# A hybrid convolution and retention layer on one core: filler work put in another order, copies and buffers split finer

## The chip, the cores and the metric

The kernel runs on one core of a Trainium2 chip. The metric is the time of one execution in microseconds on the device; the time of a kernel is the median of its runs. The kernel before took 969.17 us (three runs, 967.22 to 969.35).

## What is computed

One layer of a decoder over 1024 tokens of width 1024. A modulated RMS norm makes u; one input projection makes the inputs of a convolution branch and of a retention branch; both meet in one output projection. Cut to what matters here:

```python
u = _rmsnorm(h, norm_g[l]) * (1.0 + scale) + shift
proj = u @ w_in[l]          # conv_a, conv_bp, conv_gate, q, k, v, ret_gate
a = conv_a * jax.nn.sigmoid(conv_bp)
a = _causal_depthwise_conv(a, conv_w[l], conv_b[l])     # 31 taps
a = jax.nn.silu(_layernorm(a, conv_ln_g[l], conv_ln_b[l]))
a = a @ conv_pw[l]
y_conv = a * jax.nn.silu(conv_gate)
r = _retention_chunkwise(_rotary(q), _rotary(k) * (RET_QK_DIM ** -0.5), v)   # 4 heads
r = _head_groupnorm(r, ret_gn_g[l], ret_gn_b[l])
y_ret = r * jax.nn.silu(ret_gate)
y = jnp.concatenate([y_conv, y_ret], axis=-1) @ w_out[l]
return _rmsnorm(h + gate * y, final_g)
```

## The kernel before

All large products run in float32 as three matmuls (`mm3`, L81 to 84): each operand is split into a rounded high part (`split`, L69: a cast on ScalarE) and the remainder (L71: a subtraction on VectorE, or on GpSimd where the call names it), and high by high, high by low and low by high are added up in PSUM.

The stages, with their times in the profile:

1. Up to about 495 us: the norm and the input projection in 21 pairs of blocks, with the 31 convolution taps (L271, VectorE) behind them. The convolution's result goes to DRAM (`d_y`), and GpSimd adds it up over channels into `ysum` (L278).
2. To 535: the first values, for heads 0 and 1 (L512 to 531): eight tiles `t` of 128 tokens, each 24 matmuls of 512 columns (`values_ps`, tiles `ps_v`), with the weights split on GpSimd. The results are copied to SBUF (ScalarE for t < 6, VectorE for 6 and 7) and written to `d_v` by DMAs on GpSimd's queue.
3. To about 700: retention, four heads of four chunks (`retention`, L601 to 707). A chunk loads q, k, sg and v, splits them (tiles `qc`, `kc`, `vc`, with h and l for the parts), transposes k (`kp`), makes scores (`sp`), masks them (`sm`), splits those (`sh`, `sl`), makes outputs (`op`) and the state's update (`up`, then `state`, `sth`, `stl`), and normalises (`ob`, `rs`, `rn`, `tp`). Each step waits for another engine, so other work stands between the chunks to fill TensorE:
   - `ln_squares` (L551 to 569), the first half of the convolution's layer norm: two matmuls with a matrix of ones give the mean from `ysum` (`mu`), ScalarE makes `negmu`, and eight times a tile of `d_y` is loaded, `negmu` added (VectorE), written back, squared (ScalarE) and added to `ysum` (VectorE). Two buffers `yt` carry it.
   - `values` (L590), the second values, for heads 2 and 3: eight tiles again, from weights `w_v[1]` that come in four loads of 512 KB (`load_w`: `raw_v`, `hi_v`, `lo_v`).
   - `ln_scale` (L571 to 586): column sums of `ysum` (`var`), then `rstd` on VectorE, its power on GpSimd (L577), eight diagonal tiles `rs_d` on VectorE (L583), matmuls with ones that spread them over the partitions (`rb`, L584), and copies into `rbs`.
   - `norm_z` (L709), eight tiles: load, multiply by `rbs`, SiLU, split into `zh` and `zl`, the operand of the pointwise projection (`pointwise`, L730, tiles `ps_pw`).
4. To 961: the pointwise projection, then the output projection (L768 to 856), which adds for each tile of tokens a half that comes from retention (`w_r`) and a half that comes from the convolution (`w_c`). The first halves of two tiles run before the `w_c` weights are loaded.

After head 0 stand `ln_squares` and four tiles of second values, after head 1 the other four, then `ln_scale` and the eight `norm_z`. That is the order in the code; the order on each engine is made by a scheduler, which places each instruction by priority and readiness (loads of a chunk are raised by `LOADS_EARLIER`, taps lowered by `TAPS_LATER`); each engine then takes its instructions one after the other.

Of the kernel before, what the change touches and what calls it, by code (L numbers as in the profile page):

```python
# [7 lines left out]
F32 = mybir.dt.float32  # L8
# [4 lines left out]
P = 128  # L13
# [4 lines left out]
TT = S // P  # L18
# [2 lines left out]
EPS = 1e-6  # L21
TAPS_LATER = 3000
LOADS_EARLIER = 800
PAD_SW = 24
PAD_W = 88
CH = 256
NCH = S // CH
HALF = 512
EARLY = (8, 0, 9, 1)
HK = KT // 2  # L30
# [17 lines left out]
def hybrid_layer(ctx: ExitStack, tc: tile.TileContext, x, vec, c_row, ada_ss, ada_g, adab_g, w_e, w_s, w_p, w_v,  # L48
                 w_pw, w_out, final_g, cs, masks, kc, ident, out):
    nc = tc.nc  # L50
# [5 lines left out]
    mmp = ctx.enter_context(tc.tile_pool(name="mm", bufs=4, space=bass.MemoryType.PSUM))  # L56
# [16 lines left out]
    def load_w(src, shape, name, pool, eng=None):  # L73
        raw = pool.tile(shape, F32, tag="raw", name=f"raw_{name}", bufs=2)
        nc.sync.dma_start(raw, src)
        hi = pool.tile(shape, F32R, tag="hi", name=f"hi_{name}")
        lo = pool.tile(shape, F32R, tag="lo", name=f"lo_{name}")
        split(hi, lo, raw, eng)
        return hi, lo
# [211 lines left out]
    def values_ps(t, ws, name):  # L291

        ps = mmp.tile([P, HALF], F32, tag="mm", name=f"ps_{name}{t}")
        sl = slice(t * P, (t + 1) * P)
        for k in range(KT):
            mm3(ps, uh[k][:, sl], ul[k][:, sl], *ws[k], k == 0, k == KT - 1)
        return ps
# [77 lines left out]
    with tc.tile_pool(name="one", bufs=1, reuse_waits="tile") as op_, \  # L375
# [140 lines left out]
        ws = []  # L516
        for k in range(KT):
# [2 lines left out]
            hi, lo = (t[:, k % HK] for t in ((th[2], tl[2]), (th[3], th[4]))[k // HK])  # L520
            split(hi, lo, raw, nc.gpsimd)
            ws.append((hi, lo))
        for t in range(0, TT, 2):
            vs = op_.tile([P, 2, HALF], F32, tag="ro", name=f"vs0{t}", bufs=2)
            for i in range(2):
                ps = values_ps(t + i, ws, "v0")
                if t + 2 < TT:
                    nc.scalar.copy(vs[:, i], ps)
                else:
                    nc.vector.tensor_copy(vs[:, i], ps)  # L530
            values_out(0, t, vs, nc.gpsimd)
    one_ctx.close()
    conv_ctx.close()
# [6 lines left out]
    with tc.tile_pool(name="ret", bufs=1, reuse_waits="tile") as rp, \  # L540
# [10 lines left out]
        def ln_squares():  # L551

            negmu = const.tile([P, S], F32, tag="sig", name="negmu")
            for i in range(2):
                sl = slice(i * HALF, (i + 1) * HALF)
                mu = mmp.tile([P, HALF], F32, tag="mm", name=f"mu{i}")
                nc.tensor.matmul(mu, ones_t, ysum[:, sl], start=True, stop=True)
                nc.scalar.mul(negmu[:, sl], mu, -1.0 / D)
            for m in range(KT):
                yt = fo.tile([P, S], F32, tag="yt", name=f"ys{m}", bufs=2)  # L560
                nc.sync.dma_start(yt, d_y[m])
                nc.vector.tensor_tensor(yt, yt, negmu, op=ADD)
                nc.sync.dma_start(d_y[m], yt)
                if m == 0:
                    nc.scalar.activation(ysum, yt, AF.Square)
                else:
                    sq = fo.tile([P, S], F32, tag="xh", name=f"sq{m}", bufs=2)
                    nc.scalar.activation(sq, yt, AF.Square)
                    nc.vector.tensor_tensor(ysum, ysum, sq, op=ADD)
# [16 lines left out]
            return rbs  # L586

        w_v1 = []

        def values(ts):  # L590

            if not w_v1:
                for j in range(4):
                    hi, lo = load_w(w_v[1, j], [P, 2, HALF], f"v1{j}", wpool)
                    w_v1.extend((hi[:, i], lo[:, i]) for i in range(2))
            for t in ts:
                vs = rp.tile([P, 1, HALF], F32, tag="vs", name=f"vs{t}", bufs=3)
                nc.scalar.copy(vs[:, 0], values_ps(t, w_v1, "v1"))
                values_out(1, t, vs, nc.scalar)

        def retention(h):  # L601
# [4 lines left out]
            for c in range(NCH):  # L606
# [3 lines left out]
                def chunk(tag, src):  # L610
                    hi = rp.tile([P, 2, CH], F32R, tag=tag + "h", name=f"{tag}h{n}", bufs=2)
                    lo = rp.tile([P, 2, CH], F32R, tag=tag + "l", name=f"{tag}l{n}", bufs=2)
                    split(hi, lo, src)
                    return hi, lo

                def load_c(tag, src):
                    t = rp.tile([P, 2, CH], F32, tag=tag, name=f"{tag}{n}", bufs=2)
                    with tc.high_priority(offset=LOADS_EARLIER):
                        nc.sync.dma_start(t, src)
                    return t  # L620

                q, k = (load_c("qk"[i], d_qk[i, h][:, :, ts]) for i in range(2))
                sg = load_c("sg", d_sg[2 * h:2 * h + 2, :, ts].rearrange("d p s -> p d s"))
                vh, vl = chunk("vc", load_c("v", d_v[h // 2, :, 2 * c:2 * c + 2, h % 2 * 2 * P:(h % 2 + 1) * 2 * P]))
                if c < NCH - 1:

                    kth = rp.tile([P, 2, 2 * P], F32R, tag="kth", name=f"kth{n}", bufs=2)
# [10 lines left out]

                kh, kl = chunk("kc", k)
                qh, ql = chunk("qc", q)  # L640


                sp = rps.tile([P, 3 * P], F32, tag="sp", name=f"sp{n}")
# [76 lines left out]
        for h in range(H):  # L720
            retention(h)
            if h == 0:
                ln_squares()
            if h < 2:
                values(range(h * HK, (h + 1) * HK))
            if h == 1:
                rbs = ln_scale()
                for m in range(KT):
                    zh[m], zl[m] = norm_z(m)
    def pointwise(m):  # L730
        ps = unit(*load_w(w_pw[m], [P, KT, P], f"pw{m}", wpool), zh, zl, f"pw{m}")
        cg = fo.tile([P, S], F32, tag="xh", name=f"cgl{m}", bufs=2)
        nc.sync.dma_start(cg, d_cg[m])
        for i in range(2):
            sl = slice(i * HALF, (i + 1) * HALF)
            nc.vector.tensor_tensor(cg[:, sl], ps[i], cg[:, sl], op=MUL)
        nc.sync.dma_start(d_yc[m], cg)
# [13 lines left out]
    with tc.tile_pool(name="fin", bufs=1, reuse_waits="tile") as fp, \  # L751
# [23 lines left out]
                    not start and k == KT - 1)  # L775

        def both(t):
            return [fps.tile([P, HALF], F32, tag="o", name=f"ps_o{t}_{i}") for i in range(2)]

        def half(ps, w, y, start):  # L780
            for k in range(KT):
# [36 lines left out]

        halves2 = [slice(0, HALF), slice(HALF, D)]
        first = []  # L820
        for t in range(2):
            ps = both(t)
            half(ps, w_r, load_y(d_yr, t, "yr"), True)
            first.append(ps)
        w_c = [load_r(f, big, "big", 17) for f in range(KT)]
        for t in range(TT - 1):
            if t < 2:
                ps = first[t]
            else:
                ps = both(t)  # L830
                half(ps, w_r, load_y(d_yr, t, "yr"), True)
            half(ps, w_c, load_y(d_yc, t, "yc"), False)
            if t == 0:
                for k in range(KT):
                    gate_step(k)
                agb = fo.tile([P, D], F32, tag="yt", name="agb", bufs=2)
                nc.sync.dma_start(agb, adab_g.broadcast_to([P, D]))
                for i in range(2):
                    sl = slice(i * HALF, (i + 1) * HALF)
                    gp = mmp.tile([P, HALF], F32, tag="mm", name=f"gp{i}")  # L840
                    nc.tensor.matmul(gp, ones_t, gate[:, sl], start=True, stop=True)
                    nc.vector.tensor_tensor(gate[:, sl], gp, agb[:, sl], op=ADD)
            finish(t, [(lambda q=q: q, sl) for q, sl in zip(ps, halves2)])
# [99 lines left out]
```

## Time and profile before

| | |
|---|---|
| median of three runs | 969.17 us (967.22 to 969.35) |
| the profiled execution | 970.08 us |
| its span, first to last instruction | 968.3 us |
| mean granted TensorE clock | 0.988 |
| TensorE busy | 937.2 us (97% of the span) |
| VectorE busy | 745.3 us (77%) |
| ScalarE busy | 412.2 us (43%) |
| GpSimd busy | 389.8 us (40%) |
| moved by DMA | 154.95 MB, 160 GB/s |

The busy share is a mean over all stages. A row of a window says how much of a stretch an engine was busy and which clock TensorE was granted in it (1.00 is full speed). A row of a timeline says when an instruction began, how long it took, and in brackets how long its engine had been idle before it and which instruction of which engine released it. Matmuls are pipelined: the time from one to the next is shorter than what a row gives for one. PE is TensorE, DVE VectorE, ACT ScalarE, POOL GpSimd, SP SyncE.

### The profile page before, as it was taken

To read this page: it belongs to the slowest core of one execution; us is meant where nothing else is said; L and a number is where in the kernel's file an instruction comes from. 1 tells how busy PE (TensorE), PEld (TensorE's weight loads), DVE (VectorE), ACT (ScalarE), POOL (GpSimd) and SP (SyncE) were. 2 spreads that over 40 slices of the span, in tenths; PEclk is the share of its full clock that TensorE was granted. 3 is DMA by queue.
4 is the path that set the end of the run, shared out by engine and by line. 5 is a ranking of instruction groups with operands and counts; after the bars stand their busy time and mean duration, and the time that the engine had idled before them with its cause. 6 is when DMAs were issued, how large, how long until landed. Compare 5 with 4: busy or idle time off the path is not lost.

```text
span 968.3 us, 12531 instructions
## 1 busy us (share of the span) xinstructions
PE 937.2 (97%) x4496; PEld 784.5 (81%) x4496; DVE 745.3 (77%) x928; ACT 412.2 (43%) x676; POOL 389.8 (40%) x358
## 2 busy tenths in 40 slices
PE   7999999999999999999999899989999999999996
PEld 5788888888888888888888688877788887888886
DVE  6999989899999999999799786687875344523322
ACT  7775433433434334343430575677634333311201
POOL 3004987877887798878550111121022100000000
PEclk9999999999999999999999899989999999999998
DMA  9924242333334444443434799555775486432111
GB/s 348 331 78 133 75 144 88 118 88 104 125 121 138 133 127 132 134 141 97 154 117 163 267 332 308 179 165 200 240 290 176 157 279 221 147 106 87 65 44 44
DMA packets 84673, 154.95 MB, mean 160 GB/s; under 512 B 6657, under 2 KB 43265, under 8 KB 83330
## 3 DMA queue, kind: packets, MB, share of 16 engines
q1 hardware_dynamic: 81986, 147.07, 45.9%
q0 software_dynamic: 1040, 3.67, 1.0%
q10 hardware_dynamic: 1584, 3.41, 0.9%
q8 instruction: 35, 0.57, 0.2%
q14 instruction: 28, 0.23, 0.1%
HBM read 107.99 MB, written 46.14 MB: 159 GB/s over the span
## 4 chain that ended last, share of the span: by engine, by line
PE 78%; DVE 10%; DMA 5%; issue 3%; ACT 2%; POOL 1%; POOLq 0%; DVEq 0%; ACTq 0%
PE pa L83 7%; PE pa L84 7%; PE pa L82 7%; DVE y L271 4%; PE ps_o L83 4%; PE ps_o L84 4%; PE ps_o L82 4%; PE pb L83 4%; PE pb L82 4%; PE pb L84 4%; PE ps_pw L82 2%; PE ps_pw L84 2%; PE ps_pw L83 2%; DMA wo<-w_out 2%; PE pd L84 2%
## 5 line engine op out<-in xcount | busy, mean ns | idle before, releaser
L271 DVE SCALAR_TENSOR_TENSOR yp<-a,vec_t,yp 128x1024 f32<-128x1024 f32 x210 | 269.7, 1284 | 6.7 <-ACT yp L269 2.7
L334 POOL TENSOR_TENSOR pl<-pr,ph 128x512 fp32r<-128x512 f32 x63 | 84.7, 1345 | 59.7 <-ACT ph L333 59.5
L334 POOL TENSOR_TENSOR pl_s<-sm_s,ph_s 128x512 fp32r<-128x512 f32 x63 | 85.4, 1356 | 36.6 <-ACT ph_s L333 35.1
L333 ACT CAST ph_s<-sm_s 128x512 fp32r<-128x512 f32 x63 | 39.1, 622 | 95.8 <-PE pa L83 80.3
L333 ACT CAST ph<-pr 128x512 fp32r<-128x512 f32 x63 | 39.1, 622 | 79.7 <-PE pa L83 45.4
L806 POOL TENSOR_TENSOR fr<-fr,mhalf 128x1 f32<-128x1 f32 x7 | 3.8, 547 | 168.0 <-DVE fr L805 168.0
L691 POOL TENSOR_TENSOR rs<-mv,kc_t 128x2 f32<-128x2 f32 x16 | 6.2, 390 | 158.7 <-DVE mv L688 133.8
L82 PE MATMUL pb<-uh,ph_s 128*128 128x512 f32 x168 | 65.4, 389 | 0.0
L84 PE MATMUL pb<-uh,pl_s 128*128 128x512 f32 x168 | 65.4, 389 | 0.0
L82 PE MATMUL pa<-th,ph_s 128*128 128x512 f32 x168 | 65.4, 389 | 0.0
L83 PE MATMUL pb<-ul,ph_s 128*128 128x512 f32 x168 | 65.4, 389 | 0.0
L84 PE MATMUL pa<-th,pl_s 128*128 128x512 f32 x168 | 65.4, 389 | 0.0
L83 PE MATMUL pa<-tl,ph_s 128*128 128x512 f32 x168 | 65.4, 389 | 0.0
L346 POOL TENSOR_TENSOR sm_s<-pr,pr 128x512 f32<-128x512 f32 x42 | 57.2, 1362 | 17.3 <-DMA pr<-w_p 10.1
L83 PE MATMUL ps_pw<-zl,hi_pw 128*128 128x512 f32 x128 | 50.4, 394 | 2.2 <-DVE zl L71 2.2
L84 PE MATMUL ps_pw<-zh,lo_pw 128*128 128x512 f32 x128 | 50.6, 395 | 0.0
L82 PE MATMUL ps_pw<-zh,hi_pw 128*128 128x512 f32 x128 | 48.0, 399 | 1.9 <-ACT zh L70 1.7
L271 DVE SCALAR_TENSOR_TENSOR y<-a,vec_t,y 128x1024 f32<-128x1024 f32 x30 | 44.1, 1469 | 6.9 <-ACT y L269 6.1
L797 DVE TENSOR_TENSOR g<-ps_o,gate 128x512 f32<-128x512 f32 x14 | 9.5, 691 | 49.7 <-PE ps_o L84 49.7
L83 PE MATMUL ps_o<-wol,hi_yc 128*128 128x512 f32 x112 | 43.8, 391 | 0.1
L83 PE MATMUL ps_o<-wol,hi_yr 128*128 128x512 f32 x112 | 43.7, 393 | 0.0
L84 PE MATMUL ps_o<-woh,lo_yc 128*128 128x512 f32 x112 | 43.6, 390 | 0.0
(447 smaller groups left out, 2792.9 us busy)
## 6 DMA issues: line engine op xcount, KB each, us to landing
pr<-w_p SPq DMA_DIRECT2D x84, 256.0 KB, 2.7
aw<-ada_ss SPq DMA_DIRECT2D x8, 1024.0 KB, 8.1
d_qk<-ro SPq DMA_DIRECT2D x16, 512.0 KB, 3.3
wo<-w_out SPq DMA_DIRECT2D x16, 512.0 KB, 4.7
xt<-x SPq DMA_DIRECT2D x8, 512.0 KB, 6.9
d_sg<-o SPq DMA_DIRECT2D x16, 256.0 KB, 2.6
sg<-d_sg SPq DMA_DIRECT2D x16, 256.0 KB, 3.5
v<-d_v SPq DMA_DIRECT2D x16, 256.0 KB, 3.4
```

The costliest lines, as they stand in the source:

```text
L82: nc.tensor.matmul(ps, lh, rh, start=start, stop=False, skip_group_check=more)
L83: nc.tensor.matmul(ps, lh, rl, start=False, stop=False, skip_group_check=more)
L84: nc.tensor.matmul(ps, ll, rh, start=False, stop=stop, skip_group_check=more)
L271: nc.vector.scalar_tensor_tensor(acc, ap[:, j:j + S], col(V_CW, m * CW + j), acc, op0=MUL, op1=ADD)
L333: nc.scalar.copy(hi, src)
L334: nc.gpsimd.tensor_tensor(lo, src, hi.bitcast(F32), op=SUB)
L346: nc.gpsimd.tensor_tensor(out, a, b, op=op)
L691: nc.gpsimd.tensor_tensor(rs, mv[:, :, 1], kc_t[:, K_G2 + 2 * h:K_G2 + 2 * h + 2], op=MUL)
L797: nc.vector.tensor_tensor(g[:, :n], ps(), gate[:, sl], op=MUL)
L806: nc.gpsimd.tensor_tensor(r, r, mhalf[:, 0:1], op=ALU.pow)
```

## The change

- The first values are copied tile by tile into single tiles with five buffers (before: pairs with two), so eight writes of 256 KB take the place of four of 512 KB.
- The weights of the second values are loaded and split where the function is defined, ahead of retention, and their lo parts are made on GpSimd.
- After head 0 one tile of second values stands ahead of `ln_squares`, three behind it. After head 1 one tile stands ahead of `ln_scale`, three behind it, then come the `norm_z`.
- In a chunk the values are split after keys and queries.
- The first halves of three output tiles run ahead of the second halves' weights (before two), and the output's PSUM tiles alternate between two pools.

```diff
--- before.py
+++ after.py
@@ -21,6 +21,7 @@
 EPS = 1e-6
 TAPS_LATER = 3000
 LOADS_EARLIER = 800
+AHEAD = 3
 PAD_SW = 24
 PAD_W = 88
 CH = 256
@@ -520,14 +521,13 @@
             hi, lo = (t[:, k % HK] for t in ((th[2], tl[2]), (th[3], th[4]))[k // HK])
             split(hi, lo, raw, nc.gpsimd)
             ws.append((hi, lo))
-        for t in range(0, TT, 2):
-            vs = op_.tile([P, 2, HALF], F32, tag="ro", name=f"vs0{t}", bufs=2)
-            for i in range(2):
-                ps = values_ps(t + i, ws, "v0")
-                if t + 2 < TT:
-                    nc.scalar.copy(vs[:, i], ps)
-                else:
-                    nc.vector.tensor_copy(vs[:, i], ps)
+        for t in range(TT):
+            vs = op_.tile([P, 1, HALF], F32, tag="plb", name=f"vs0{t}", bufs=5)
+            ps = values_ps(t, ws, "v0")
+            if t + 2 < TT:
+                nc.scalar.copy(vs[:, 0], ps)
+            else:
+                nc.vector.tensor_copy(vs[:, 0], ps)
             values_out(0, t, vs, nc.gpsimd)
     one_ctx.close()
     conv_ctx.close()
@@ -586,13 +586,12 @@
             return rbs
 
         w_v1 = []
+        for j in range(4):
+            hi, lo = load_w(w_v[1, j], [P, 2, HALF], f"v1{j}", wpool, nc.gpsimd)
+            w_v1.extend((hi[:, i], lo[:, i]) for i in range(2))
 
         def values(ts):
 
-            if not w_v1:
-                for j in range(4):
-                    hi, lo = load_w(w_v[1, j], [P, 2, HALF], f"v1{j}", wpool)
-                    w_v1.extend((hi[:, i], lo[:, i]) for i in range(2))
             for t in ts:
                 vs = rp.tile([P, 1, HALF], F32, tag="vs", name=f"vs{t}", bufs=3)
                 nc.scalar.copy(vs[:, 0], values_ps(t, w_v1, "v1"))
@@ -621,7 +620,7 @@
 
                 q, k = (load_c("qk"[i], d_qk[i, h][:, :, ts]) for i in range(2))
                 sg = load_c("sg", d_sg[2 * h:2 * h + 2, :, ts].rearrange("d p s -> p d s"))
-                vh, vl = chunk("vc", load_c("v", d_v[h // 2, :, 2 * c:2 * c + 2, h % 2 * 2 * P:(h % 2 + 1) * 2 * P]))
+                v = load_c("v", d_v[h // 2, :, 2 * c:2 * c + 2, h % 2 * 2 * P:(h % 2 + 1) * 2 * P])
                 if c < NCH - 1:
 
                     kth = rp.tile([P, 2, 2 * P], F32R, tag="kth", name=f"kth{n}", bufs=2)
@@ -638,6 +637,7 @@
 
                 kh, kl = chunk("kc", k)
                 qh, ql = chunk("qc", q)
+                vh, vl = chunk("vc", v)
 
 
                 sp = rps.tile([P, 3 * P], F32, tag="sp", name=f"sp{n}")
@@ -720,13 +720,16 @@
         for h in range(H):
             retention(h)
             if h == 0:
+                values(range(1))
                 ln_squares()
-            if h < 2:
-                values(range(h * HK, (h + 1) * HK))
+                values(range(1, HK))
             if h == 1:
+                values(range(HK, HK + 1))
                 rbs = ln_scale()
+                values(range(HK + 1, TT))
                 for m in range(KT):
                     zh[m], zl[m] = norm_z(m)
+
     def pointwise(m):
         ps = unit(*load_w(w_pw[m], [P, KT, P], f"pw{m}", wpool), zh, zl, f"pw{m}")
         cg = fo.tile([P, S], F32, tag="xh", name=f"cgl{m}", bufs=2)
@@ -775,7 +778,8 @@
                     not start and k == KT - 1)
 
         def both(t):
-            return [fps.tile([P, HALF], F32, tag="o", name=f"ps_o{t}_{i}") for i in range(2)]
+            pool, tag = (fps, "o") if t % 4 < 2 else (mmp, "mm")
+            return [pool.tile([P, HALF], F32, tag=tag, name=f"ps_o{t}_{i}") for i in range(2)]
 
         def half(ps, w, y, start):
             for k in range(KT):
@@ -818,13 +822,13 @@
 
         halves2 = [slice(0, HALF), slice(HALF, D)]
         first = []
-        for t in range(2):
+        for t in range(AHEAD):
             ps = both(t)
             half(ps, w_r, load_y(d_yr, t, "yr"), True)
             first.append(ps)
         w_c = [load_r(f, big, "big", 17) for f in range(KT)]
         for t in range(TT - 1):
-            if t < 2:
+            if t < AHEAD:
                 ps = first[t]
             else:
                 ps = both(t)
```

What this does to the order on the engines, at three places. Line numbers behind L21 shift by one and more.

On TensorE at the end of the first values (`ps_v`, lines 82 to 84), before:

```order
L84 MATMUL ps_v_4582<-th_671,ul_109 128x512
L557 MATMUL mu_5096<-ysum,ones_t 128x512
L557 MATMUL mu_5099<-ysum,ones_t 128x512
L633 MATMUL kp_4665<-ident_t,k_4653 128x128 x2
L82 MATMUL sp_4682<-qch_4678,kch_4674 128x256
L83 MATMUL sp_4682<-qcl_4679,kch_4674 128x256
```

and in the changed kernel, there and where `mu` stands now:

```order
L85 MATMUL ps_v_4590<-th_671,ul_109 128x512
L632 MATMUL kp_4693<-ident_t,k_4685 128x128 x2
L83 MATMUL sp_4714<-qch_4706,kch_4702 128x256
L84 MATMUL sp_4714<-qcl_4707,kch_4702 128x256
...
L83 MATMUL ps_v_5128<-hi_v_4665,uh_96 128x512
L557 MATMUL mu_5156<-ysum,ones_t 128x512
L557 MATMUL mu_5159<-ysum,ones_t 128x512
L83 MATMUL ps_v_5217<-hi_v_4659,uh_94 128x512
```

The mean's two matmuls moved from right behind the first values to 54 rows later, into the first two tiles of second values; transposed keys and scores of the first chunk follow the first values directly.

On ScalarE at the same place (`vs`: copies of first values), before:

```order
L528 COPY vs_4501<-ps_v_4528 128x512
L558 ACTIVATE negmu<-mu_5096 128x512
L558 ACTIVATE negmu<-mu_5099 128x512
L70 CAST vch_4659<-v_4657 128x512
L70 CAST qch_4678<-q_4651 128x512
L70 CAST kch_4674<-k_4653 128x512
```

and in the changed kernel:

```order
L528 COPY vs_4533<-ps_v_4534 128x512
L71 CAST vch_4710<-v_4689 128x512
L71 CAST qch_4706<-q_4683 128x512
L71 CAST kch_4702<-k_4685 128x512
L635 ACTIVATE kth_4691<-kp_4693,kc_t 128x256
L71 CAST qch_4816<-q_4793 128x512
```

The casts of the first chunk follow the copies directly; `negmu` stands 17 rows further down, behind the casts of three chunks and of the first two pieces of weights.

On TensorE around the variance, before (`ps_v_5823` is the eighth tile of second values; the other columns of `var` follow among the next 40 rows):

```order
L82 MATMUL ps_v_5823<-hi_v_5176,uh_101 128x512
L83 MATMUL ps_v_5823<-lo_v_5177,uh_101 128x512
L84 MATMUL ps_v_5823<-hi_v_5176,ul_109 128x512
L574 MATMUL var<-ones_t,ysum 128x1 x5
L82 MATMUL up_5476<-vch_5412,kth_5416 128x256
```

and in the changed kernel (`ps_v_5816` is the sixth tile):

```order
L85 MATMUL op_5352<-vch_5329,sl_5349 128x256
L574 MATMUL var<-ones_t,ysum 128x1 x8
L83 MATMUL up_5362<-vch_5329,kth_5310 128x256
...
L632 MATMUL kp_5422<-ident_t,k_5414 128x128 x2
L584 MATMUL rb_5787<-rs_d_5788,ones_t 128x128
L584 MATMUL rb_5787<-rs_d_5791,ones_t 128x128
L83 MATMUL op_5462<-sth_5377,qch_5435 128x256
...
L584 MATMUL rb_5801<-rs_d_5802,ones_t 128x128
L83 MATMUL ps_v_5816<-hi_v_4659,uh_94 128x512
```

All eight columns of the variance now stand behind the fifth tile of second values, in the output of head 1's first chunk, and the sixth to eighth tile stand behind the `rb` matmuls.

## Rows read from the trace of the kernel before

**Rows 1.** Windows of 25 us, TensorE: span, its length, busy (instructions), granted clock, DMA share, GB/s.

```profile
500.00:525.00 25.00, 25.00 (x112) 1.00 0.61 198
525.00:550.00 25.00, 20.27 (x92) 0.86 0.48 177
550.00:575.00 25.00, 25.00 (x151) 1.00 0.98 345
...
625.00:650.00 25.00, 19.45 (x126) 0.80 0.54 174
650.00:675.00 25.00, 22.51 (x140) 1.00 0.63 210
675.00:700.00 25.00, 22.88 (x132) 1.00 0.67 222
...
800.00:825.00 25.00, 24.79 (x105) 1.00 0.66 213
```

**Rows 2.** One window of 3 us, TensorE, same columns.

```profile
543.00:546.00 3.00, 2.01 (x10) 0.52 0.67 224
```

**Rows 3.** Timeline of TensorE at A: start, us, line, out<-in, count, idle before it <-releaser.

```profile
534.38 0.39 PE L84 MATMUL ps_v<-th,ul 128*128 128x512 f32 x1
...
536.13 1.98 PE L557 MATMUL mu<-ysum,ones_t 128*128 128x512 f32 x4 [1.35 <-POOL ysum L278]
...
537.95 0.38 PE L633 MATMUL kp<-ident_t,k 128*128 128x128 f32 x2
...
540.34 0.38 PE L82 MATMUL sp<-qch,kch 128*128 128x256 f32 x1 [2.01 <-ACT kch L70]
...
543.99 0.55 PE L82 MATMUL sp<-qch,kch 128*128 128x256 f32 x1 [1.15 <-DVE sm L650]
```

**Rows 4.** Timeline of ScalarE at A.

```profile
537.29 0.60 ACT L558 ACTIVATE negmu<-mu 128x512 f32<-128x512 f32 x1 [12.77 <-PE mu L557]
```

**Rows 5.** Timeline of VectorE at A.

```profile
534.81 0.69 DVE L530 COPY vs<-ps_v 128x512 f32<-128x512 f32 x1 [1.35 <-PE ps_v L84]
...
539.28 0.69 DVE L71 TENSOR_TENSOR vcl<-v,vch 128x512 fp32r<-128x512 f32 x1 [3.78 <-ACT vch L70]
...
540.49 0.68 DVE L71 TENSOR_TENSOR kcl<-k,kch 128x512 fp32r<-128x512 f32 x1
```

**Rows 6.** Timeline of GpSimd at A.

```profile
533.70 2.37 POOL L278 TENSOR_TENSOR ysum<-ysum,y 128x1024 f32<-128x1024 f32 x1
```

**Rows 7.** Timeline of TensorE at B.

```profile
629.35 0.58 PE L82 MATMUL op<-sth,qch 128*128 128x256 f32 x1 [1.30 <-ACT sth L70]
...
630.81 0.58 PE L83 MATMUL op<-stl,qch 128*128 128x256 f32 x1 [0.88 <-DVE stl L71]
...
647.29 0.44 PE L633 MATMUL kp<-ident_t,k 128*128 128x128 f32 x2 [1.08 <-DVE ktl L637]
```

**Rows 8.** By line, variance to rb: count, ns min/median/max, first and last start.

```profile
L574 PE MATMUL var<-ones_t,ysum x16: 166/250/251, 620.9 to 627.8; 128*128 128x1 f32 x16
...
L577 POOL TENSOR_TENSOR rstd<-rstd,mhalf x1: 1887/1887/1887, 631.5 to 631.5; 128x8 f32<-128x8 f32 x1
...
L584 PE MATMUL rb<-rs_d,ones_t x16: 273/276/324, 638.8 to 643.4; 128*128 128x128 f32 x16
```

**Rows 9.** By line, the squares: same columns.

```profile
L562 DVE TENSOR_TENSOR ys<-ys,negmu x8: 1208/1216/1225, 543.8 to 587.2; 128x1024 f32<-128x1024 f32 x8
...
L569 DVE TENSOR_TENSOR ysum<-ysum,sq x7: 1215/1221/1226, 548.1 to 590.6; 128x1024 f32<-128x1024 f32 x7
```

**Rows 10.** Timeline of GpSimd, splits of the first values' weights.

```profile
497.28 8.68 POOL L71 TENSOR_TENSOR th<-wv,th 128x512 fp32r<-128x512 f32 x4 [9.13 <-PE pa L84]
```

**Rows 11.** Timeline of VectorE, taps beside those splits and after them.

```profile
495.51 11.54 DVE L271 SCALAR_TENSOR_TENSOR y<-a,vec_t,y 128x1024 f32<-128x1024 f32 x6
...
511.77 18.45 DVE L271 SCALAR_TENSOR_TENSOR y<-a,vec_t,y 128x1024 f32<-128x1024 f32 x14
```

**Rows 12.** Page, costliest groups: line, engine, forms, count | busy us, mean ns | idle before.

```profile
L334 POOL TENSOR_TENSOR pl<-pr,ph 128x512 fp32r<-128x512 f32 x63 | 84.7, 1345 | 59.7 <-ACT ph L333 59.5
```

## The prediction, made before the changed kernel was run

> **What bounds the kernel now.** I read three views, in this order. First TensorE's busy time in stretches of 25 us: outside the first microseconds and the tail TensorE is the bound, and a full stretch reads 25.00 of 25 [rows 1]. Only five stretches shown fall short: 4.73 us are missing in 525–550, 5.55 in 625–650, 2.49 and 2.12 in the two after it, 0.21 in 800–825, together 15.1 us. Secondly the granted clock in the same rows: it is 0.86 in 525–550 and 0.80 in 625–650, 1.00 elsewhere. [...] So about 22 us in all are there to be won, at two seams: from the first values to retention (A, 534–550) and behind the variance (B, 626–651) with its aftermath (C, 651–700). Thirdly the timelines of each engine at A and B, to see which wait ends last.
>
> At A the last matmul of the first values starts at 534.38 and the mean's matmuls (mu) wait 1.35 us for ysum and take 1.8 us; scores then wait 2.01 us for the cast kch, and the next chunk 1.15 us for sm [rows 3]. The cast waits since negmu stands ahead of it on ScalarE, which itself waited 12.77 us for mu [rows 4]; VectorE's vcl waited 3.78 us for that cast [rows 5]. ysum is a GpSimd add of 2.37 us [rows 6]. So one row of ones-times-ysum, which nobody needs yet, holds three engines. At B retention waits for sth, stl and ktl (1.30, 0.88, 1.08 us), with no other TensorE work in the queue [rows 7]. The variance's columns go through TensorE from 620.9 to 627.8, the power on GpSimd takes 1.89 us, and the rb matmuls come from 638.8 on [rows 8].
>
> **The change, part by part,** each as what is left of the loss before (A 4.73 + 3, B 5.55 + 4, C 4.61, output 0.21).
>
> *A, idle.* In the new order scores come straight behind the first values, mu 54 rows later, behind the first second-values matmuls. The three chunk casts go ahead of negmu on ScalarE and so are done while TensorE still computes the first values. What is late next is VectorE: its second copy of first values starts at 534.81 and takes 0.69 us, then come vcl, qcl, kcl at a pitch of 0.60 [rows 5]. So kcl ends near 537.3, where it ended at 541.17 before: 3.9 us earlier. Scores wait about 1.9 us for VectorE, as they do for kch now; the sm wait of 1.15 stays, and I allow 0.7 for what follows in that chain, without a row for it. I leave 3.8 us of idle time (bounds 2 and 4.7: nothing beyond the three waits that remain, or all as now).
>
> *A, clock.* It was down at 543 to 546 [rows 2], behind the first two waits, 3.4 us of the 9 before. The gaps of the new order lie as close together, so I let it fall again, at 2.9 us; bounds 0 and 3. The mean's own 1.8 us are moved, not saved.
>
> *The weights sooner.* Four loads of 512 KB, eight cast halves and four lo splits leave the stretch from 545 on. The lo splits, 1.22 us each on VectorE like its other operations of that shape [rows 9], go to GpSimd: 4.9 us off VectorE, 9.6 us onto GpSimd by the 2.37 us of another add of the same shape [rows 6]. The first two are needed by 545; their loads no longer wait for anything later than about 527, so they are ready by 543. The other two stand behind them and are needed six or more matmuls later. GpSimd has nothing else there. SyncE's queue gets these loads ahead of the first chunks' third and fourth tiles, so the third chunk's keys may land only near 560, where TensorE wants them at about 562. And both engines slow each other: taps ran six in 11.54 us (1.92 each) while GpSimd split the first weights, 14 in 18.45 (1.32 each) without it, and four of GpSimd's splits took 8.68 us, 2.17 each [rows 10, 11]. I charge 1 us for all this, bounds 0 and 5.
>
> [...]
>
> *The squares behind one tile of values.* Eight steps of load, add, write, square, sum: from the first add at 543.8 to the end of the last sum near 591.8, 48.1 us [rows 9]. That time is set by transfers: the DMA share is 0.98 in 550–575 [rows 1]. Nothing waited for it, since the variance came 29 us later [rows 8]. Now it starts at about 548, when mu has gone behind the first tile, and ends at 596 at the same pace. Without the 2 MB of weights (6 us at the 345 GB/s of that stretch, half of it in the chain's way) it ends at 593.
>
> *The variance behind five tiles.* The new order has 120 matmuls of 512 columns (0.223 us each, from 112 in 25 us [rows 1]), 127 of 256 (half of that), 48 of 128 columns (no faster, 0.11) and mu's 1.8 us between the first chunk's outputs and the variance: 48 us. From near 543.5 that is 591.6, and 592.6 with the 1 us above. So TensorE and the chain arrive together; I charge 1 us of waiting, bounds 0 and 10.
>
> *B.* Then come 21 matmuls of 256 columns and a few transposes, 2.8 us, before the first rb matmul, which wants variance, rstd, GpSimd's 1.89 us power, and the rs_d products. Before, variance to rb took from 628 to 638.8 [rows 8], mostly behind VectorE's queue. With two or three instructions of 0.7 ahead on VectorE, the power and the two short steps around it, it is some 5.8 us, so 3 us idle, bounds 1.5 (nothing ahead) and 8 (as before). Three tiles of values (16.3 us) now stand behind rb and cover rbs and the first norm_z; these covered nothing when they stood ahead of the variance. The sth, stl and ktl waits go with them. Clock: 3 us of gap between full stretches on both sides; gaps of 2.49 us in 650–675 left the clock at 1.00 [rows 1], so 0; bounds 0 and 4.
>
> *C.* The eight z tiles start some 25 us sooner, but they need the yt buffers and VectorE and ScalarE as before, and TensorE's projections now also come when three value tiles are spent. I leave 4 us of 4.61; bounds 1.5 and 7.
>
> *Copies of the first values one by one, the value split behind keys and queries, three tiles ahead in the output.* Eight DMA issues of 0.53 us on GpSimd's idle queue replace four, beside full TensorE: 0. The third first half meets a stage where 0.21 us are missing at most [rows 1]: 0.
>
> **Sum.** Left over: 3.8 + 2.9 + 1 + 1 + 3 + 0 + 4 + 0.2 = 15.9 us, of 22.1 before: 6.2 us less. The profiled execution took 970.08 us, 0.91 above the median of 969.17. So 963.9 against it, and 963.0 for the median.
>
> **Rivals.**
> - *The clock stays up and the gaps close.* If 3.8 us of gaps don't bring the clock down at A, the chain is in time and the value tiles cover the z chain: left over 3.8 + 1.5 + 2.5, gain 14, 955. For it: the gaps are shorter than before. Against: they lie just as dense at A, and C's tiles are limited by buffers that haven't changed.
> - *The gain goes back in clock.* Gaps of 3 to 4 us at both seams bring the clock down at both (2.9 + 3) and the early loads cost 3 instead of 1: gain near 1, 968, not to be told from before. For it: it fell twice here after such gaps.
> - *Slower: the squares chain becomes the bound.* The variance stands in TensorE's queue 28 us sooner, and all behind it waits in order. Place: the wait for ysum at about 593. Each microsecond that the chain ends later than TensorE arrives is lost. From 7 us of lateness on, the gain above is gone, and with the clock down after such a gap (3 us) already from 4. If VectorE and the transfers, now with more per microsecond, make the chain 56 us rather than 45, it ends at 604: 11 us of wait and 3 of clock in place of the 1 charged, 13 against a gain of 6: 7 slower than before, 976. For it: the DMA share of 0.98 and only 29 us of slack, all spent. Against: 2 MB fewer in that stretch.
> - *Each GpSimd split stops VectorE for its whole length:* 9.6 - 4.9 = 4.7 us more of VectorE's time, while VectorE is what scores wait for: gain 1.5, 967.7. For it: the slowed taps [rows 10, 11]; against: they were slowed by less. [...]
>
> **How the numbers follow.** The forecast's case 0.50 (959 to 967: one term or two at an end of its bounds); the clock stays up 0.13; back in clock 0.17; slower 0.14; exclusion 0.06. The range leaves out the better half of the second case and most of the slower one: 956 to 971.5. A measurement of this kernel can tell 0.2% (1.9 us) from no change: faster is all of the first two, a part of the last and a few of the third, 0.68; same 0.17; slower 0.15.
>
> **What would show it.** Right: no row of mu ahead of the first sp, kcl ending near 537, variance at about 594 with an idle time of a microsecond, a gap of about 3 us ahead of rb, and windows 625–650 full. Wrong: a variance row with many microseconds waiting for VectorE's ysum; clock below 1 behind it; a second-values matmul waiting for GpSimd's lo_v; taps at 1.9 us near 535.

## The result, and the profile after

The changed kernel takes 959.71 us (median of four runs, 958.77 to 961.18) against 969.26 for the kernel before: a ratio of 0.9896, 95% interval 0.9880 to 0.9913. It is faster by 1.0%, clear of the 0.2% that a measurement of this kernel can tell. The forecast was 963.0 with a range of 956.0 to 971.5 and a chance of 0.68 for faster. The profiled execution took 958.77 us with a span of 957.0, 11.3 less than before.

First TensorE's windows of the changed kernel, with the columns of [rows 1]:

```profile
525.00:550.00 25.00, 22.65 (x106) 0.86 0.59 203
...
550.00:575.00 25.00, 23.08 (x134) 0.93 0.82 284
...
625.00:650.00 25.00, 25.00 (x149) 1.00 0.76 251
...
650.00:675.00 25.00, 23.80 (x146) 1.00 0.60 194
...
675.00:700.00 25.00, 25.00 (x145) 1.00 1.02 364
...
800.00:825.00 25.00, 22.06 (x93) 1.00 0.53 170
```

Against [rows 1], the seam from first values to retention has 2.35 us idle instead of 4.73 and the same clock of 0.86. The seam behind the variance, 5.55 us idle at a clock of 0.80, is gone altogether: 25.00 at 1.00. Of the 4.61 idle behind it 1.20 are left. Two losses are new: 1.92 us idle and a clock of 0.93 in 550–575, where before it was full, and 2.94 us idle in 800–825, where 0.21 were. In idle time that makes −2.4, −5.6, −3.4, +1.9 and +2.7: 6.7 us less. By the clock it makes some 3.5 us less at the second seam. Before, the clock there was 0.50 from 628.4 to 638.6, with TensorE busy for 7.9 us of that; matmuls of 256 columns start 0.214 us apart at 0.50 (547.1 to 549.5) and 0.119 at 1.00 (639.9 to 641.1), so I estimate that 0.44 of that busy time is lost. In 550–575 it makes 1.6 more: 3.4 us of work at 0.50 from 557.5 to 560.9, with matmuls of 512 columns 0.43 us apart there and 0.23 behind it. Together that is 8.6 of the 11.3 us; no row here places the rest.

TensorE's timeline of the changed kernel shows the waits that end these idle times:

```profile
536.47 0.39 PE L84 MATMUL sp<-qcl,kch 128*128 128x256 f32 x1 [1.83 <-DVE qcl L72]
...
540.21 0.55 PE L83 MATMUL sp<-qch,kch 128*128 128x256 f32 x1 [0.30 <-DVE sm L650]
...
557.47 0.62 PE L632 MATMUL kp<-ident_t,k 128*128 128x128 f32 x2 [1.92 <-DVE ktl L636]
...
810.68 0.74 PE L83 MATMUL ps_o<-woh,hi_yc 128*128 128x512 f32 x2 [1.63 <-ACT woh L71]
...
811.94 0.50 PE L84 MATMUL ps_o<-wol,hi_yc 128*128 128x512 f32 x1 [0.52 <-DVE wol L72]
...
820.46 0.96 PE L83 MATMUL ps_o<-woh,hi_yc 128*128 128x512 f32 x3 [0.67 <-ACT woh L71]
```

At A scores now wait for VectorE's qcl (1.83 us, [rows 3] had 2.01 for kch), as forecast, and the wait for sm shrank from 1.15 to 0.30. The wait for ktl at 557.47 and those for the output's weights (woh, wol) are the two new losses. By line, squares to rb, columns as in [rows 8, 9]:

```profile
L562 DVE TENSOR_TENSOR ys<-ys,negmu x8: 1184/1218/1224, 551.5 to 590.0; 128x1024 f32<-128x1024 f32 x8
...
L569 DVE TENSOR_TENSOR ysum<-ysum,sq x7: 1210/1216/3073, 557.3 to 594.4; 128x1024 f32<-128x1024 f32 x7
...
L574 PE MATMUL var<-ones_t,ysum x16: 164/250/250, 598.5 to 600.1; 128*128 128x1 f32 x16
...
L577 POOL TENSOR_TENSOR rstd<-rstd,mhalf x1: 1642/1642/1642, 600.6 to 600.6; 128x8 f32<-128x8 f32 x1
...
L584 PE MATMUL rb<-rs_d,ones_t x16: 270/275/324, 603.4 to 611.9; 128*128 128x128 f32 x16
```

The squares' sums run from 551.5 until 595.6, the variance comes at 598.5 and waits for nothing; rb follows 3.3 us behind the last column of the variance, where before it took 11.0 us [rows 8].

### The profile page after: what moved, and what is told of

The parts are those of the page before. It is cut to its first block, busy times and chain, and to the rows that moved or that the text cites. A ratio compares the mean times of both kernels' runs of the same rounds, so it can differ in the third digit from the quotient of the medians.

```text
span 957.0 us, 12534 instructions
## 1 busy us (share of the span) xinstructions
PE 932.5 (97%) x4496; PEld 780.8 (82%) x4496; DVE 747.2 (78%) x924; ACT 411.1 (43%) x676; POOL 405.1 (42%) x366
## 4 chain that ended last, share of the span: by engine, by line
PE 84%; DMA 7%; DVE 4%; ACT 2%; issue 2%; POOL 1%; SPq 0%; POOLq 0%; DVEq 0%; ACTq 0%
PE pa L84 8%; PE pa L85 8%; PE pa L83 8%; DMA wo<-w_out 4%; PE pb L84 4%; PE pb L83 4%; PE pb L85 4%; PE ps_o L83 4%; PE ps_o L84 4%; PE ps_o L85 4%; PE ps_v L84 3%; PE ps_v L83 3%; PE ps_v L85 3%; PE ps_pw L84 2%; PE ps_pw L85 2%; PE ps_pw L83 2%
## 5 line engine op out<-in xcount | busy, mean ns | idle before, releaser
L83 PE MATMUL ps_o<-woh,hi_yc 128*128 128x512 f32 x112 | 43.0, 392 | 2.4 <-ACT woh L71 2.3
```

Of the source, the lines that this page charges most:

```text
L83: nc.tensor.matmul(ps, lh, rh, start=start, stop=False, skip_group_check=more)
```

## The experiments

All ratios are to the kernel before on the same chip. Two theories of what took some of the gain back were formed from this profile: that GpSimd's splits of the weights stop VectorE (A in experiment 1), and that the output's weights are the new bound (called A in experiment 2 and C from experiment 5 on). In experiments 1 to 4 each expectation uses the letters A and B anew; from 5 on C to H keep their meaning.

**1. The weights' lo parts on VectorE again.**

```diff
-            hi, lo = load_w(w_v[1, j], [P, 2, HALF], f"v1{j}", wpool, nc.gpsimd)
+            hi, lo = load_w(w_v[1, j], [P, 2, HALF], f"v1{j}", wpool)
```

> The changed kernel with the lo parts of the second values' weights made on VectorE again. Theory A (GpSimd's splits stop VectorE: in the changed kernel nb took 2.30 us instead of 0.15, one sum 3.07 instead of 1.22, and TensorE then waited 1.92 us for ktl and ran at half clock for 3.4 us): the wait and the low clock in 550 to 575 go, 956 us against 959.7 of the changed kernel. Rival B (VectorE is what the scores wait for, and 4.9 us of work come back to it): no better or slower, 960 to 965, with new waits for VectorE between 540 and 570.

Measured: 959.35 us, ratio 0.9893 (0.9869 to 0.9917). No difference to the changed kernel, and in neither forecast's range. Its windows and the one long wait in them (the profiled execution took 962.33, the longest of the six):

```profile
550.00:575.00 25.00, 25.00 (x149) 1.00 0.85 283
...
575.00:600.00 25.00, 23.03 (x150) 1.00 0.91 308
```

```profile
594.32 0.38 PE L84 MATMUL sp<-qcl,kch 128*128 128x256 f32 x1 [1.93 <-DVE qcl L72]
```

The wait and the low clock in 550–575 did go, as A said; a wait of 1.93 us for VectorE's qcl came instead, as B said, but at 594 and not between 540 and 570. What A describes is there (sl, 2.42 us beside a split in the changed kernel, takes 0.55 here), and removing it gains nothing. That the 4.9 us of work which VectorE takes back are what matches its price is likely, but no run shows it.

**2. Two tiles ahead in the output.** `AHEAD = 2` in place of 3.

> The changed kernel with two tiles' first halves ahead in the output instead of three. Theory A (the output starts 14 us sooner than before, but the last of its weights are cast only some 5 us sooner, so that TensorE catches up with the loads; the third tile covers 11 us of that): the idle time of 2.8 us around 810 to 821 grows to 6 or more, 963 to 966. Rival B (the third tile's own load delays the weights, and that makes the 2.8 us): the idle time falls to 0.2 as before, 957.

Measured: 961.52 us, ratio 0.9911 (0.9888 to 0.9935). The direction of this expectation's A, but some 1.5 us (0.15%) instead of 3 to 6, and the intervals overlap with the changed kernel's. The wait stands at the first half now:

```profile
787.63 2.08 PE L83 MATMUL ps_o<-woh,hi_yr 128*128 128x512 f32 x4 [3.44 <-ACT woh L71]
...
805.76 0.62 PE L85 MATMUL ps_o<-woh,lo_yr 128*128 128x512 f32 x2
...
806.21 0.39 PE L83 MATMUL ps_o<-woh,hi_yr 128*128 128x512 f32 x1
```

The run does not take the third tile away, though. The two PSUM pools stay, and with them 19 of the 48 matmuls of the third tile's first half (the last two rows are of them) ran between 802 and 818, ahead of the end of the first two tiles; 800–825 is full. In experiment 4, with one pool, two of them ran before 826.6. So the second pool does part of what the third tile does, and no run separates the two: experiments 6 and 9 bring both.

**3. The old order of squares and variance, all else as changed.**

```diff
             if h == 0:
-                values(range(1))
                 ln_squares()
-                values(range(1, HK))
+                values(range(HK))
             if h == 1:
-                values(range(HK, HK + 1))
+                values(range(HK, TT))
                 rbs = ln_scale()
-                values(range(HK + 1, TT))
```

> The changed kernel with squares and variance put back to their old places (squares ahead of the first tile of second values, variance behind the eighth); all else as changed. Theory A (the order carries the gain): the idle time and the low clock behind the variance (5.5 and 4 us) come back, 966 to 970, about as before. Rival B (weights ahead of time, and on GpSimd, carry half of it): 963 to 965.

Measured: 978.24 us, ratio 1.0088 (1.0063 to 1.0113): slower than before, beyond both theories. So the order is needed, and something among the rest costs time without it.

**4. The two moves alone, on the kernel before.** The reverse of the diff above, applied to the kernel before.

> The kernel before with the two moves alone: squares behind one tile of second values, variance behind five. Theory A (the order carries the gain): 957 to 961, windows 625 to 650 full at clock 1.00. Rival B (without the weights ahead of time the first tile of second values isn't ready when the order wants it, and TensorE waits for it): 964 or more, with a wait for hi_v or lo_v near 546.

Measured: 967.11 us, ratio 0.9976 (0.9958 to 0.9994). Only a quarter of the gain. The seam behind the variance did close (25.00 us busy at clock 1.00 in 625–650), as A had it, and B's wait for the second values' weights behind 546 isn't there; yet the time is B's. Up to the end of the projections the moves did win 12 us (771.3 against 783.2), in spite of 2.55 us idle at a clock of 0.93 in 575–600. Most of that went again in the output:

```profile
775.00:800.00 25.00, 21.02 (x85) 1.00 0.79 252
...
800.00:825.00 25.00, 23.96 (x99) 1.00 0.59 190
```

```profile
789.02 1.20 PE L82 MATMUL ps_o<-woh,hi_yr 128*128 128x512 f32 x4 [2.69 <-ACT woh L70]
...
795.85 1.20 PE L82 MATMUL ps_o<-woh,hi_yr 128*128 128x512 f32 x4 [0.73 <-ACT woh L70]
```

TensorE waits for woh, the high parts of the output's weights. This is what made theory C.

**5. Four raw buffers for the output's weights.** In the changed kernel, every second weight takes a buffer that has come free:

```diff
-            raw = fp.tile([P, D], F32, tag="rw", name=f"wo{f}", bufs=2)
+            rpool, rtag = (fp, "rw") if f % 2 else (fo, "yt")
+            raw = rpool.tile([P, D], F32, tag=rtag, name=f"wo{f}", bufs=2)
```

> The changed kernel with the raw tiles of the output's weights in four buffers instead of two (every second one takes the free yt buffers). Theory C (the output's weights are the new bound: load, cast and split of one take some 6.6 us in two buffers, 3.3 us each, and TensorE, 12 us earlier than before, catches up with them): the gaps of 2.9 us in 800 to 825 go, 956.5 to 958. Rival D (the transfers themselves are late, or the loads can't begin before retention's buffers are free, whatever their number): the same gaps, 959 to 961.

Measured: 955.99 us, ratio 0.9860 (0.9845 to 0.9875), half a microsecond below C's range. C holds. The casts of the 16 weights, by line (count, ns min/median/max, first and last start), in the changed kernel:

```profile
L71 ACT CAST woh<-wo x16: 1044/1052/1056, 766.0 to 819.4; 128x1024 fp32r<-128x1024 f32 x16
```

and with four buffers:

```profile
L71 ACT CAST woh<-wo x16: 1042/1052/1059, 759.0 to 799.1; 128x1024 fp32r<-128x1024 f32 x16
```

From first to last cast 53.4 us with two buffers and 40.1 with four, 3.6 and 2.7 for a weight, so D falls. Two of the sixteen loads also moved up to 664 and 667; the others begin at 762.8, no sooner than in the changed kernel (761.6), though retention's last matmul starts at 756.9 here; so part of the gain may be those two loads'. The gain lies behind the projections: they end at 768.6 here and at 768.8 in the changed kernel, and from there to the end are 185.3 us here and 188.2 there. What waits in 800–825 now is the gate, whose own loads used those yt buffers:

```profile
821.81 1.55 PE L846 MATMUL gp<-gate,ones_t 128*128 128x512 f32 x3 [0.95 <-DVE gate L751]
```

**6. The two moves and the third tile, on the kernel before.** Experiment 4 with `range(3)` and `t < 3` in place of 2, and the two pools for the PSUM tiles.

> The kernel before with the two moves and the third tile ahead in the output. The two moves alone gave 967.1, with 5 us idle in 775 to 825. Theory C (what the moves win is lost again at the output's weights): the idle time there falls to about 3 and the time to 962 to 965. Rival E (the weights of the second values, ahead of time, make the difference between 967.1 and 959.7): 966 to 968.

Measured: 961.88 us, ratio 0.9910 (0.9893 to 0.9927), 0.1 us below C's range; the idle time in 775–825 is 3.2 us. C holds: 0.66% or 6 us less than the moves alone, and nearly nine tenths of the whole change's gain. What is left for the other parts (early weights, first values copied one by one, the values' split behind keys and queries) is 0.14%, within the intervals; the last two were not run by themselves.

**7. The second values' weights late and on VectorE, all else as changed.**

```diff
-        for j in range(4):
-            hi, lo = load_w(w_v[1, j], [P, 2, HALF], f"v1{j}", wpool, nc.gpsimd)
-            w_v1.extend((hi[:, i], lo[:, i]) for i in range(2))
...
+            if not w_v1:
+                for j in range(4):
+                    hi, lo = load_w(w_v[1, j], [P, 2, HALF], f"v1{j}", wpool)
+                    w_v1.extend((hi[:, i], lo[:, i]) for i in range(2))
```

> The changed kernel with the second values' weights loaded at their first use and split on VectorE, as before; all else as changed. Theory C: 960 to 963, since the order and the third tile carry the gain. Rival E (the weights ahead of time are the part that the moves need): 965 to 967, with waits behind 546 for those weights or for VectorE.

Measured: 959.82 us, ratio 0.9898 (0.9882 to 0.9914), just below C's range. In the new order the weights ahead of time, with their splits on GpSimd, give nothing and cost nothing. E falls.

**8. The weights ahead of time alone, on the kernel before.** The reverse of the diff of 7.

> The kernel before with the second values' weights ahead of time and their lo parts on GpSimd, nothing else. The changed kernel with the old order took 978.2, nine more than before. Rival F (weights ahead of time and GpSimd's splits are a loss where the squares come first): 973 to 978. Theory C (they are nearly free, and what cost nine there is another part): 968 to 971.

Measured: 979.51 us, ratio 1.0103 (1.0087 to 1.0120), above F's range. F holds in direction: under the old order this part costs 1.0%, which is what experiment 3 had lost. Where it goes is only seen in part. The window behind the variance in this kernel:

```profile
625.00:650.00 25.00, 19.73 (x132) 0.88 0.61 210
```

5.27 us idle, like before [rows 1]; more idle time is spread thinly over 575 to 775. The projections end 3.7 us later than before (786.9 against 783.2), and from there to the end are 190.6 us instead of 185.1, 5.5 more. That larger part goes with the loads of the output's weights: in SyncE's queue they stand behind the write of the seventh projection, at 777.6, where before they stood behind that of the sixth, at 765.0. Why the scheduler put them one projection later was not taken apart.

**9. The third tile alone, on the kernel before.** As in 6, without the moves.

> The kernel before with the third tile ahead in the output, nothing else. The prediction gave this part 0. Theory C (the third tile only fills what the output's weights leave empty, and before the change they left 0.2 us empty): 968 to 970, as before. Rival G (the third tile wins its 5 us, the difference between the two moves alone and the two moves with it, whatever stands ahead): 963 to 966.

Measured: 967.77 us, ratio 0.9985 (0.9970 to 0.9999): 0.15%, too little to be told from no change. The prediction's 0 for this part holds on the kernel before, and G falls: the same edit is worth 6 us behind the moves.

**10. The variance alone back behind the eighth tile, all else as changed.** The second half of the diff of 3.

> The changed kernel with the variance alone put back behind the eighth tile of second values; the squares stay behind one tile. The prediction had the seam behind the variance give 6.5 of the 6.2 us and the first seam 1. If so: 966 to 975, with several us idle and a low clock in 625 to 650. Rival H (the first seam carries the gain, and the variance's place matters little): 960 to 963.

Measured: 971.64 us, ratio 1.0023 (1.0007 to 1.0039), 12 us above the changed kernel. The variance's place carries the gain, H falls. Against experiment 3 (1.0088), where the squares are back in their old place too, that place is worth another 0.65%, 6 us; the squares alone put back were not run. The two windows with the seam (the profiled execution took 975.73, the longest of the twelve):

```profile
625.00:650.00 25.00, 21.14 (x129) 0.80 0.56 186
...
675.00:700.00 25.00, 23.10 (x131) 0.93 0.72 242
```

3.86 us idle at 0.80, and 1.90 at 0.93, both full at 1.00 in the changed kernel.

**11. Four raw buffers and two tiles ahead.** Experiment 5 with `AHEAD = 2`.

> The changed kernel with four raw buffers for the output's weights and two tiles ahead. Theory C (the third tile and the buffers cover the same lateness): with the weights in time the third tile is worth little, 956 to 958.5. Rival G (the third tile has a worth of its own): 960 to 963.

Measured: 969.41 us, ratio 1.0003 (0.9989 to 1.0017). Neither. The edit made a wait of its own:

```profile
824.45 2.08 PE L846 MATMUL gp<-gate,ones_t 128*128 128x512 f32 x2 [10.89 <-DVE gate L751]
```

The weights now hold the yt buffers through which the gate is loaded, and without the third tile nothing covers it: 10.89 us. The run says nothing on what it was made for.

**12. Four raw buffers, the second values' weights late.** Edits 5 and 7 together.

> The changed kernel with four raw buffers for the output's weights, and the second values' weights loaded at their first use and split on VectorE as before. If the weights ahead of time give nothing and GpSimd's splits cost 1 to 3 us between 540 and 560: 954 to 956. If they save as much elsewhere (the output began at 769 with them, later without): 956 to 958.

Measured: 954.65 us, ratio 0.9853 (0.9830 to 0.9877). The fastest of all, 4 to 5 us below the changed kernel; against experiment 5 (955.99) the intervals overlap, so the two cases of the expectation are not told apart. The output is full, and 1.6 us at a clock of 0.98 remain near 594:

```profile
575.00:600.00 25.00, 23.41 (x151) 0.98 0.88 307
...
800.00:825.00 25.00, 25.00 (x109) 1.00 0.67 214
```

## Why the prediction was right

Its direction, its place and its mechanism at A held; the size came out at 10 us where 6 were forecast. Term by term some 13 us are left over in the profile where the forecast has 15.9: A's idle time, the squares, B and C came out 8 us lower, the early weights and the output 5 us higher. That the sum lies as close as it does is in part luck, since these errors cancel. And the forecast rested on a part that it had put at 0: without the third tile and its pool the moves gave 2.3 us (experiment 4), with them 9 (experiment 6).

- *A, idle, 3.8.* Measured 2.35. The chain was as described: kcl ended at 537.0 (537.3 forecast), scores waited 1.83 us for VectorE. The sm wait that was to stay shrank to 0.30, since VectorE had emptied its queue when the scores ended; but they ended late because they ran at a clock of 0.50 from 537.1 on. In experiments 1, 4, 5, 6 and 7, where the first chunk's scores of 256 columns followed one another at 0.11 to 0.13 us, not 0.21, the sm wait is 1.14 or 1.15 as forecast, and the window has 3.2 to 3.3 us idle.
- *A, clock, 2.9.* The clock did fall, to 0.50 from 537.1 to 543.9, 6.5 us of it busy, so about 2.9 at the 0.44 estimated above. Right, and with it the rival of a clock that stays up is out for this seam. The rival that the gain goes back in clock is out too: at the second seam it stayed at 1.00. No run shows the 3 and 4 us that the list of losses sets down for the clock at A and B; the trace of before shows 6.0 and 7.9 us of busy time at 0.50, about 2.7 and 3.5 lost by the same estimate.
- *Weights sooner, 1 (bounds 0 and 5).* In the profile the loss in 550–575 is 1.92 idle and 1.6 of clock, 3.5 us. It is no fixed price: experiment 5 has the same early weights and the same splits on GpSimd, and there the wait is 0.56 and the clock 1.00:

```profile
550.00:575.00 25.00, 24.45 (x152) 1.00 0.83 291
```

  Experiments 1 and 7 show that leaving the splits or the whole part out gains nothing: another wait for VectorE, of 1.93 and 2.21 us, stands at 594. As a part of the change it is 0. That it costs 10 us without the moves (experiment 8) was in no one's forecast here.
- *Squares and variance, 1 (bounds 0 and 10).* 0. The chain took 44 us (45 forecast) and ended at 595.6 (593). TensorE came at 598.5 (592.6): the first chunk's outputs began 1.3 us later (544.8 for 543.5), 550–575 lost 3.5, and the same matmuls took 2 us longer than the 48 reckoned, against 1 us already charged. They met within 3 us, with the chain ahead. The rival that ends slower needed the chain 4 us behind TensorE; it was 3 ahead.
- *B, 3 idle.* This step failed. It put two or three instructions of 0.7 us on VectorE ahead of rstd and rs_d, which made the chain from the variance to rb 5.8 us long, 3 more than the 2.8 of retention's matmuls that cover it. VectorE's rows show one such instruction, ahead of rs_d only:

```profile
600.37 0.17 DVE L576 TENSOR_SCALAR rstd<-var 128x8 f32<-128x8 f32 x1
...
601.90 0.69 DVE L674 COPY state<-up 128x512 f32<-128x512 f32 x1 [1.36 <-PE up L85]
```

  It ran beside the end of GpSimd's power (600.6 to 602.3), so the chain from the last column of the variance to rb took 3.3 us, and 3.2 us of retention's matmuls, which stand between the two on TensorE, covered it all. Experiment 10 prices this move: 12 us.
- *C, 4 (bounds 1.5 and 7).* This step failed too: 1.20. The multiplications by rbs run from 613.2 to 661.8 instead of 644.5 to 685.3. The z chain is slower (49 us instead of 41), but it begins 31 us sooner, beside the three tiles of values, and the projections catch up with it only once, at 653.6.
- *Output, 0.2.* This step failed the other way: 2.94 in the changed kernel. The prediction looked at the output of before, saw it full, and gave the third tile 0. It did not ask for how long the full stretch would last if TensorE came there 12 us earlier. The last of the output's weights was cast at 824.9 in the kernel before:

```profile
L70 ACT CAST woh<-wo x16: 1047/1050/1057, 769.4 to 824.9; 128x1024 fp32r<-128x1024 f32 x16
```

and in the kernel with the moves alone:

```profile
L70 ACT CAST woh<-wo x16: 1044/1051/1055, 769.0 to 822.1; 128x1024 fp32r<-128x1024 f32 x16
```

The first of those loads was issued at 765.0 before and 764.1 with the moves alone, and from there the last cast was 58 to 60 us away, although TensorE came 12 us sooner. What held that first load last is SyncE's queue. It stands right behind another load, which waits for the write of a projection's result; before:

```profile
764.67 0.32 SPq L733 DMA_DIRECT2D cgl<-d_cg  x1
765.04 0.90 SPq L759 DMA_DIRECT2D wo<-w_out  x2
```

and in the changed kernel:

```profile
761.20 0.33 SPq L794 DMA_DIRECT2D h<-x  x1
761.59 1.02 SPq L762 DMA_DIRECT2D wo<-w_out  x2
```

It did not wait for retention's end: retention's last chunks run among the projections, not up to about 700 as the list of stages has it, and its last matmul (tp) starts at 767.4 before, after that load was issued (in the changed kernel the second load waits 0.5 us for it). From the last cast to the end of the span are 143.4 us before and 142.8 with the moves alone; with the third tile and the second pool 137.6 in the changed kernel (819.4 to 957.0) and 138.9 in experiment 6, and 141.2 with the second pool alone (experiment 2). So the kernel before already stood at the edge of this limit, with 0.2 us to show for it, and the moves, which let the last projection end 12 us sooner (771.3 for 783.2), brought the end forward by only 3.4. The third tile with its pool moves the limit by 4 to 6 us.

Of the rivals, the exclusion of VectorE by GpSimd is there in the trace (nb took 2.30 us for 0.16 beside a split), and its price is not: experiments 1 and 7 gain nothing by taking it out. Its rows stand in the last section.

## What to carry to other kernels

A stretch that is full may be just full: before you price what an earlier arrival is worth, look there for the chain that supplies it (here load, cast and split through two buffers, begun behind another load in the same queue) and ask how late it ends, not whether anything waits for it today. Parts of a change can have opposite signs without each other (here −2 for the moves, +10 for the weights and −1.5 for the third tile alone, −10 for all together), so leave parts out of the whole as well as adding them one by one. A short chain through three engines, here the variance with 3.3 us, cost nothing where tiles of independent work stood behind it, and 12 us where they had been used up ahead of it (experiment 10).

## What the runs showed of the hardware

Beside GpSimd's splits, four VectorE instructions that read two operands from SBUF took 2.23 to 3.07 us instead of 0.16 to 1.22, and two that read one from PSUM took their usual 0.56 and 0.47. GpSimd's timeline in the changed kernel, two splits of 128x1024 each:

```profile
541.44 5.04 POOL L72 TENSOR_TENSOR lo_v<-raw_v,hi_v 128x1024 fp32r<-128x1024 f32 x2 [5.13 <-ACT hi_v L71]
...
554.64 4.69 POOL L72 TENSOR_TENSOR lo_v<-raw_v,hi_v 128x1024 fp32r<-128x1024 f32 x2
```

and VectorE's beside them:

```profile
541.80 2.42 DVE L72 TENSOR_TENSOR sl<-sm,sh 128x384 fp32r<-128x384 f32 x1 [0.86 <-ACT sh L71]
...
544.33 0.56 DVE L650 TENSOR_TENSOR sm<-sp,mask 128x384 f32<-128x384 f32 x1
...
544.80 2.23 DVE L72 TENSOR_TENSOR qcl<-q,qch 128x512 fp32r<-128x512 f32 x1
...
554.72 2.30 DVE L695 SCALAR_TENSOR_TENSOR nb<-mv,rs 128x2 f32<-128x2 f32 x1 [0.91 <-POOL rs L694]
...
556.94 0.47 DVE L636 SCALAR_TENSOR_TENSOR ktl<-kp,kc_t,kth 128x256 fp32r<-128x256 f32 x1
...
557.34 3.07 DVE L569 TENSOR_TENSOR ysum<-ysum,sq 128x1024 f32<-128x1024 f32 x1
```

sl (0.55 us before) took 2.42, qcl (0.68) 2.23, nb (of two columns, 0.16 elsewhere) 2.30, and the sum of the squares 3.07 instead of 1.22. The four splits end at 543.81, 546.48, 557.00 and 559.33, and these four instructions 0.41, 0.55, 0.02 and 1.08 us behind them, in each case 0.13 or 0.14 less than their own length. Between them sm (one operand in PSUM) took its 0.56 and ktl (the same) its 0.47, beside a running split. The taps of [rows 11] did the same: the four that ran beside the splits of [rows 10] took 2.20 us each and ended 1.1 behind the end of a split, while the two ahead of them took 1.28, so the 1.92 of the prediction is a mean of both kinds. And yet taking the splits off GpSimd gained the whole kernel nothing (959.35 us in experiment 1 and 959.82 in experiment 7, against 959.71).
